# The root of the norms' column sums: one GpSimd power instruction in place of a bit trick and three Newton steps

## The chip, the cores and the metric

The kernel runs on one core of one Trainium2 chip. The metric is the device time of one execution in microseconds (us); lower is better. The core's engines work at the same time and wait for each other through semaphores: PE (TensorE, matrix products), DVE (VectorE), ACT (ScalarE), POOL (GpSimd) and SP (SyncE), which issues most transfers. POOL issues transfers too.

## The reference, cut to what matters

One inference step of a decoder layer: a prompt of 2048 tokens and 64 sample tokens, model width 1024, FFN width 2816, all in fp32. Four RMS norms frame the two sub-layers; each needs, for every token, the inverse root of the mean square of its 1024 values.

```python
def rmsnorm(x, g):
    xf = x.astype(jnp.float32)
    y = xf * lax.rsqrt(jnp.mean(xf * xf, axis=-1, keepdims=True) + EPS)
    return (y * g.astype(jnp.float32)).astype(x.dtype)

def layer(x, ...):
    xn = rmsnorm(x, g_pre_mix)
    proj = xn @ w_in                      # dilated attention and GLA heads
    ...
    x = x + rmsnorm(mixed, g_post_mix)
    f, conv_new = conv_ffn(rmsnorm(x, g_pre_ffn), conv_buf, w_up, conv_w, conv_b, w_down)
    x = x + rmsnorm(f, g_post_ffn)
```

## The kernel before

Values lie transposed: the 1024 features on 128 partitions in 8 tiles, tokens along the free axis. Every product of fp32 values is done as three matmuls on high and low parts (names ending in h and l, or hi and lo; `split`, L71, makes the low part on DVE or POOL).

The program has three parts. The sweeps (0 to about 600 us) make the projections, in four chunks `c` of 512 tokens, with the GLA heads' work woven in. Attention follows, to about 1100 us. The tail takes chunks of 528 tokens: output projection `wo`, the generator `post` (two norms for each chunk), then the FFN (`ffn`, `strassen`, `down`) and the last norm (`final` for chunks 0 to 2, `final_end` for the two halves of chunk 3, which end the program).

A norm is made in `rms_bcast`:

- the squares are summed over the 8 tiles into `ssq`, on DVE or POOL;
- PE multiplies each 128 tokens of `ssq` with a column of ones (L128; L130 adds a second summand): `pn`, one column of up to 5 values on each partition;
- `rms_cols` takes the root: DVE makes `av` (L103, named rca) = mean + EPS, then a first guess by a bit trick (L104), then three Newton steps. With `eng="v"` the steps run on DVE (L113 to L115, three instructions each); with `eng="p"` on POOL (L107 to L110, four each). The result is named rcy;
- PE transposes rcy, broadcast to 128 columns (L145): `pb`, a row of factors for all partitions. ACT or DVE copies it to SBUF (L61, L63), or it is read in place (L1734).

There are 17 such norms. Eleven have `pin=True` and took their Newton steps on POOL: two for each chunk in `post`, one each in `final` for chunks 0 to 2. Pinned means that the transposes of L145 have a fixed place in PE's order, behind a given matmul. Six have `pin=False` and took them on DVE: four in `norm_pre` (chunks 0 to 3 of the sweeps) and two in `final_end`. In chunk 0 of the sweeps the column rcy is also copied by DVE into `y0` (L668, L669), which scales later tiles. The GLA head norm in `gla_out` calls `rms_cols` by itself, always on DVE, and keeps doing so.

The order of instructions on each engine is set when the program is built, by a scheduler that works with its own estimate of durations, under the places fixed by hand (`after`, `gate`). Each engine then runs its list in order: whatever stands behind a waiting instruction waits too.

Of the kernel before, what the change touches and what calls it, by code (L numbers as in the profile page):

```python
# [10 lines left out]
F32 = mybir.dt.float32  # L11
# [3 lines left out]
ALU = mybir.AluOpType  # L15
AX = mybir.AxisListType

D = 1024
# [18 lines left out]
class Layer:  # L37
# [13 lines left out]
    def consts(self):  # L51
        nc = self.nc
        self.cp = self.ctx.enter_context(self.tc.tile_pool(name="const", bufs=1))
        self.ident = self.cload("ident", [128, 128])
        self.ones = self.cp.tile([128, 1], F32, name="c_ones")
        nc.vector.memset(self.ones, 1.0)
        self.gv = self.cload("gvec", [128, 4, KT])

    def evac(self, out, in_, eng):
# [38 lines left out]
    def rms_cols(self, ps, n, inv, nb, pool, name, eng="v"):  # L98
        nc = self.nc
        av = pool.tile([128, nb], F32, name=self.n(name + "a"), tag="rc_a", bufs=2)  # L100
        y = pool.tile([128, nb], F32, name=self.n(name + "y"), tag="rc_y", bufs=2)
        z = pool.tile([128, nb], F32, name=self.n(name + "z"), tag="rc_z", bufs=2)
        nc.vector.tensor_scalar(av[:n], ps, inv, EPS, op0=ALU.mult, op1=ALU.add)  # L103
        nc.vector.tensor_scalar(y[:n].bitcast(I32), av[:n].bitcast(I32), -0.5, 1597463007.0, op0=ALU.mult, op1=ALU.add)  # L104
        if eng == "p":
            for _ in range(3):
                nc.gpsimd.tensor_tensor(z[:n], y[:n], y[:n], op=ALU.mult)  # L107
                nc.gpsimd.tensor_tensor(z[:n], z[:n], av[:n], op=ALU.mult)
                nc.gpsimd.tensor_scalar(z[:n], z[:n], -0.5, 1.5, op0=ALU.mult, op1=ALU.add)
                nc.gpsimd.tensor_tensor(y[:n], z[:n], y[:n], op=ALU.mult)  # L110
            return y
        for _ in range(3):
            nc.vector.tensor_tensor(z[:n], y[:n], y[:n], op=ALU.mult)  # L113
            nc.vector.scalar_tensor_tensor(z[:n], z[:n], -0.5, av[:n], op0=ALU.mult, op1=ALU.mult)
            nc.vector.scalar_tensor_tensor(y[:n], z[:n], 1.5, y[:n], op0=ALU.add, op1=ALU.mult)  # L115
        return y

    def rms_bcast(self, ssq, w, out, pool, psum, tag, shape=(128, 512), bufs=None, gap=2, lead=0, eng="a", pin=False, more=None):
        nc = self.nc
        for _ in range(lead):  # L120
            yield
        nb, n = -(-w // 128), 128
        o = [min(128 * j, w - 128) for j in range(nb)]
        ps = psum.tile(list(shape), F32, name=self.n("pn"), tag=tag, bufs=bufs)
        if len(shape) == 3:
            ps = ps[:, 0, :]
        for j in range(nb):
            self.pnmm = nc.tensor.matmul(ps[:n, j:j + 1], ssq[:, o[j]:o[j] + n], self.ones, start=True, stop=more is None)  # L128
            if more is not None:
                nc.tensor.matmul(ps[:n, j:j + 1], more[:, o[j]:o[j] + n], self.ones, start=False, stop=True)  # L130
            if pin:
                self.after(self.pnmm, self.lastmm)
            self.gate("n", self.pnmm)
        y = self.rms_cols(ps[:n, :nb], n, 1.0 / D, nb, pool, "rc", "p" if pin else "v")
        self.ycol = y
        for _ in range(gap):
            yield
        for g in range(0, nb, 4):
            pb = psum.tile(list(shape), F32, name=self.n("pb"), tag=tag, bufs=bufs)
            self.pbt = pb  # L140
            if len(shape) == 3:
                pb = pb[:, 0, :]
            for j in range(g, min(g + 4, nb)):
                pm = self.lastmm
                self.pbmm = nc.tensor.transpose(pb[:, o[j] - o[g]:o[j] - o[g] + n],  # L145
                                                y[:n, j:j + 1].to_broadcast([n, 128]), self.ident)
                if pin:
                    self.after(self.pbmm, pm)
            m = o[j] - o[g] + n
            if out is not None:  # L150
                self.evac(out[:, o[g]:o[g] + m], pb[:, :m], eng)
# [1861 lines left out]
```

## Time and profile before

| What | Value |
|---|---|
| time, median of 3 runs | 2807.63 us (2795.0 to 2810.9) |
| profiled execution | 2800.35 us; its span, first to last instruction, 2798.5 us |
| granted TensorE clock over the span | 0.98 |
| PE busy | 2682.2 us (96%) |
| DVE busy | 1841.5 us (66%) |
| ACT busy | 1269.1 us (45%) |
| POOL busy | 593.4 us (21%) |

PE is busy nearly all the time, so the idle pieces of PE, some 116 us in all (2798.5 less 2682.2), are where a change on another engine can show. The profile names for each idle piece the instruction that ended it. Rows of a timeline read: start in us, length in us, engine, line, operation, output<-input, size, count, and in brackets the idle time of that engine just before, with what ended it. Buffer numbers are left out of names there.

### The profile page before, as it was taken

To read this page: it belongs to the slowest core of one execution; us is meant where nothing else is said; L and a number is where in the kernel's file an instruction comes from. 1 tells how busy PE (TensorE), PEld (TensorE's weight loads), DVE (VectorE), ACT (ScalarE), POOL (GpSimd) and SP (SyncE) were. 2 spreads that over 40 slices of the span, in tenths; PEclk is the share of its full clock that TensorE was granted. 3 is DMA by queue.
4 is the path that set the end of the run, shared out by engine and by line. 5 is a ranking of instruction groups with operands and counts; after the bars stand their busy time and mean duration, and the time that the engine had idled before them with its cause. 6 is when DMAs were issued, how large, how long until landed. Compare 5 with 4: busy or idle time off the path is not lost. (4 is left out here: it accounts for less than half of the span.)

```text
span 2798.5 us, 58530 instructions
## 1 busy us (share of the span) xinstructions
PE 2682.2 (96%) x22203; PEld 2538.9 (91%) x22203; DVE 1841.5 (66%) x4578; ACT 1269.1 (45%) x2959; POOL 593.4 (21%) x741
## 2 busy tenths in 40 slices
PE   7999999999989998998999998999999999999997
PEld 6889899788778887998899998999999999999997
DVE  7667655444357777466999888676577766666666
ACT  6535433333257776344554444434244333343332
POOL 3424242443333666013000011000020000200001
PEclk9999999999999999998999999999999999999998
DMA  8755446789798764367578677886698875976654
GB/s 302 258 177 181 168 129 208 269 329 361 269 211 174 185 165 141 102 231 254 195 275 297 224 273 291 290 297 223 211 333 282 298 237 198 328 255 215 219 186 147
DMA packets 283594, 656.82 MB, mean 235 GB/s; under 512 B 31841, under 2 KB 81633, under 8 KB 281265
## 3 DMA queue, kind: packets, MB, share of 16 engines
q1 hardware_dynamic: 253008, 574.66, 61.1%
q0 software_dynamic: 13216, 46.56, 5.1%
q10 hardware_dynamic: 17088, 31.86, 3.1%
q8 instruction: 175, 2.87, 0.4%
q14 instruction: 107, 0.87, 0.1%
HBM read 509.02 MB, written 143.94 MB: 233 GB/s over the span
## 5 line engine op out<-in xcount | busy, mean ns | idle before, releaser
L68 ACT ACTIVATE ws<-wr 128x512 fp32r<-128x512 f32 (+1 forms) x482 | 292.9, 616 | 432.4 <-PE pfe L1585 139.1
L90 PE MATMUL pfd<-hh,ws 128*128 128x264 f32 x2816 | 476.9, 286 | 8.3 <-ACT ws L68 6.7
L90 PEld LDWEIGHTS pfd<-hh,ws 128*128 128x128 f32 x2816 | 401.4, 189 | 11.2 <-ACT ws L68 8.6
L71 DVE TENSOR_TENSOR ws<-wr,ws 128x512 fp32r<-128x512 f32 (+1 forms) x482 | 320.0, 670 | 135.8 <-ACT ws L68 131.0
L90 PE MATMUL pfd<-hl,ws 128*128 128x264 f32 x1408 | 303.7, 285 | 0.0
L1585 PE MATMUL pfa<-xh,ws 128*128 128x264 f32 x1496 | 292.8, 287 | 6.8 <-ACT ws L68 2.4
L1585 PE MATMUL pfe<-xh,ws 128*128 128x264 f32 x1496 | 288.6, 285 | 4.2 <-DVE u L1572 2.9
L1585 PE MATMUL pfd<-xh,ws 128*128 128x264 f32 x1408 | 288.0, 285 | 2.8 <-DVE up L1572 2.4
L1585 PEld LDWEIGHTS pfa<-xh,ws 128*128 128x128 f32 x1496 | 237.3, 190 | 8.7 <-ACT p L1574 2.9
L1585 PEld LDWEIGHTS pfe<-xh,ws 128*128 128x128 f32 x1496 | 235.9, 189 | 4.9 <-DVE u L1572 3.3
L398 PE MATMUL pv<-wh,xh 128*128 128x256 f32 (+1 forms) x816 | 234.1, 287 | 1.1 <-DVE th L695 1.1
L1585 PEld LDWEIGHTS pfd<-xh,ws 128*128 128x128 f32 x1408 | 230.7, 189 | 3.8 <-DVE up L1572 3.0
L398 PE MATMUL pv<-wl,xh 128*128 128x256 f32 (+1 forms) x816 | 232.0, 284 | 0.0
L398 PE MATMUL pv<-wh,xl 128*128 128x256 f32 (+1 forms) x816 | 231.9, 284 | 0.0
L90 PEld LDWEIGHTS pfd<-hl,ws 128*128 128x128 f32 x1408 | 226.8, 189 | 0.1
L1534 POOL DMA_DIRECT2D xl<-d_xst x52 | 28.6, 550 | 894.5 <-PE pfe L1585 866.0
L1826 ACT ACTIVATE ass<-ass,aml 128x256 f32<-128x256 f32 (+1 forms) x384 | 173.6, 454 | 89.8 <-DVE aml L1822 88.6
L1585 PE MATMUL pfd<-xl,ws 128*128 128x264 f32 x704 | 200.2, 285 | 0.0
L90 PE MATMUL pq<-xh,wh 128*128 128x512 f32 (+2 forms) x480 | 175.4, 373 | 10.2 <-ACT xh L236 7.7
L1613 DVE TENSOR_TENSOR acc<-acc,pfd 128x264 f32<-128x264 f32 x304 | 116.7, 424 | 91.0 <-PE pfd L90 90.9
L1585 PE MATMUL pfe<-xl,ws 128*128 128x264 f32 x616 | 175.4, 285 | 0.0
L1585 PE MATMUL pfa<-xl,ws 128*128 128x264 f32 x616 | 175.2, 284 | 0.0
(341 smaller groups left out, 6691.4 us busy)
## 6 DMA issues: line engine op xcount, KB each, us to landing
ws<-d_wst SPq DMA_DIRECT2D x248, 512.0 KB
wr<-in_wu SPq DMA_DIRECT2D x114, 512.0 KB
d_wst<-ws SPq DMA_DIRECT2D x88, 512.0 KB
wr<-in_wd SPq DMA_DIRECT2D x160, 256.0 KB
wr<-in_wt SPq DMA_DIRECT2D x60, 512.0 KB
wh<-d_wbs SPq DMA_DIRECT2D x35, 512.0 KB
wl<-d_wbs SPq DMA_DIRECT2D x35, 512.0 KB
skp<-in_ckt SPq DMA_DIRECT2D x16, 1024.0 KB
```

Of the source, the lines that this page charges most:

```text
L68: h = nc.scalar.activation(hi, src, AF.Copy)
L71: return h, (nc.gpsimd if lo_eng == "p" else nc.vector).tensor_tensor(lo, src, hi.bitcast(F32), op=ALU.subtract)
L90: mm = nc.tensor.matmul(o, ww[:, k, :], xx[:, s0:s0 + n], start=(k == order[0] and i == 0), stop=(k == order[-1] and i == 2))
L398: mm = nc.tensor.matmul(ps[:m, :256], x[:, t0:t0 + m], w[:, k % 4, :], start=(k == 0 and i == 0), stop=(k == KT - 1 and i == 2))
L1534: self.nc.gpsimd.dma_start(t.bitcast(F32), xo[i, z])
L1585: self.lastmm = nc.tensor.matmul(bank[:, :H], w[:, ww, k, :], xx, start=new and k == 0 and j == 0, stop=k == 3 and j == 2, skip_group_chec ...
L1613: nc.vector.tensor_tensor(acc[m][:, s0:s0 + n], acc[m][:, s0:s0 + n], pz, op=ALU.add)
L1826: ex = nc.scalar.activation(ssb[:, sc:sc + nk], ssb[:, sc:sc + nk], AF.Exp, bias=self.ml[:, idx, h:h + 1], scale=-1.0, accum_out=self.ml[: ...
```

## The change

`consts` gets a tile of minus one half, 128x5, set once by DVE. In `rms_cols` the path for `eng="p"` becomes a single POOL instruction, av to the power of minus one half; the bit trick on DVE and the twelve POOL instructions of that path are gone. In `rms_bcast` all 17 norms now take this path, also the six that took DVE's. `z` is still allocated and not used there. Behind the edit every line number is lower by 2 (L145 becomes L143); ahead of it higher by 2 (L71 becomes L73); av moves from L103 to L105, and the power instruction is the new L107.

```diff
@@ consts
         nc.vector.memset(self.ones, 1.0)
+        self.mhalf = self.cp.tile([128, 5], F32, name="c_mhalf")
+        nc.vector.memset(self.mhalf, -0.5)
@@ rms_cols
         nc.vector.tensor_scalar(av[:n], ps, inv, EPS, op0=ALU.mult, op1=ALU.add)
+        if eng == "p":
+            nc.gpsimd.tensor_tensor(y[:n], av[:n], self.mhalf[:n, :nb], op=ALU.pow)
+            return y
         nc.vector.tensor_scalar(y[:n].bitcast(I32), av[:n].bitcast(I32), -0.5, 1597463007.0, op0=ALU.mult, op1=ALU.add)
-        if eng == "p":
-            for _ in range(3):
-                nc.gpsimd.tensor_tensor(z[:n], y[:n], y[:n], op=ALU.mult)
-                nc.gpsimd.tensor_tensor(z[:n], z[:n], av[:n], op=ALU.mult)
-                nc.gpsimd.tensor_scalar(z[:n], z[:n], -0.5, 1.5, op0=ALU.mult, op1=ALU.add)
-                nc.gpsimd.tensor_tensor(y[:n], z[:n], y[:n], op=ALU.mult)
-            return y
         for _ in range(3):
@@ rms_bcast
-        y = self.rms_cols(ps[:n, :nb], n, 1.0 / D, nb, pool, "rc", "p" if pin else "v")
+        y = self.rms_cols(ps[:n, :nb], n, 1.0 / D, nb, pool, "rc", "p")
```

Three places in the engines' lists show what moves. The first is DVE in the first norm of the sweeps (chunk 0); wl is the low part of a weight tile, pb the transposed factors, gq and gk GLA tiles that are scaled by them. Before:

```order
L113 TENSOR_TENSOR rcz_292<-rcy_291 128x4
L71 TENSOR_TENSOR wl_459<-wr_456,wh_458 128x1024
L114 SCALAR_TENSOR_TENSOR rcz_292<-rcz_292,rca_290 128x4
L115 SCALAR_TENSOR_TENSOR rcy_291<-rcz_292,rcy_291 128x4
L668 COPY y_345<-rcy_291 128x4
L669 TENSOR_SCALAR y_345<-rcy_291 128x4
L63 COPY rb_284<-pb_338 128x512
L672 SCALAR_TENSOR_TENSOR gq_258<-pq_259,rb_284 128x512
```

The same place in DVE's list after the change, from av on:

```order
L105 TENSOR_SCALAR rca_292<-pn_287 128x4
L73 TENSOR_TENSOR wl_409<-wr_406,wh_408 128x1024
L666 COPY y_338<-rcy_293 128x4
L667 TENSOR_SCALAR y_338<-rcy_293 128x4
L65 COPY rb_286<-pb_331 128x512
L670 SCALAR_TENSOR_TENSOR gq_260<-pq_261,rb_286 128x512
L670 SCALAR_TENSOR_TENSOR gk_305<-pq_306,rb_286 128x512
L614 TENSOR_TENSOR lr_343<-plr_196,rb_286 128x512
L73 TENSOR_TENSOR wl_452<-wr_449,wh_451 128x1024
```

The ten instructions of the root are gone from DVE, the copy into y now waits for POOL, and one weight split that stood among the Newton steps has moved behind lr.

The second place is POOL in `post` of chunk 2, second norm, behind a run of transfers (L1534) that POOL issues for the FFN. Before, with the four instructions of a Newton step, which follow twice more:

```order
L1534 DMA xh_16445<-d_xst 128x528
L1534 DMA xl_16446<-d_xst 128x528
L107 TENSOR_TENSOR rcz_16350<-rcy_16349 128x5
L108 TENSOR_TENSOR rcz_16350<-rcz_16350,rca_16348 128x5
L109 TENSOR_SCALAR rcz_16350<-rcz_16350 128x5
L110 TENSOR_TENSOR rcy_16349<-rcz_16350,rcy_16349 128x5
```

The same place in POOL's list after the change, where this norm and the next two take one row each:

```order
L1532 DMA xh_16339<-d_xst 128x528
L1532 DMA xl_16340<-d_xst 128x528
L107 TENSOR_TENSOR rcy_16255<-rca_16254,c_mhalf 128x5
L107 TENSOR_TENSOR rcy_16424<-rca_16423,c_mhalf 128x5
L107 TENSOR_TENSOR rcy_17508<-rca_17507,c_mhalf 128x5
L1532 DMA xl_21001<-d_xst 128x528
```

Nothing is moved across the transfers; the norm's place among them is the same.

The third place is DVE at the end of the program, where the last half of `final_end` takes its norm. Before, with the first of the three Newton steps:

```order
L1734 SCALAR_TENSOR_TENSOR acc_31930<-acc_31930,c_gvec,pb_35552 128x264
L103 TENSOR_SCALAR rca_35648<-pn_35641 128x3
L104 TENSOR_SCALAR rcy_35649<-rca_35648 128x3
L113 TENSOR_TENSOR rcz_35650<-rcy_35649 128x3
L114 SCALAR_TENSOR_TENSOR rcz_35650<-rcz_35650,rca_35648 128x3
L115 SCALAR_TENSOR_TENSOR rcy_35649<-rcz_35650,rcy_35649 128x3
```

After:

```order
L1732 SCALAR_TENSOR_TENSOR acc_31764<-acc_31764,c_gvec,pb_35377 128x264
L105 TENSOR_SCALAR rca_35473<-pn_35466 128x3
L1732 SCALAR_TENSOR_TENSOR acc_31526<-acc_31526,c_gvec,pb_35484 128x264
L1732 SCALAR_TENSOR_TENSOR acc_31560<-acc_31560,c_gvec,pb_35484 128x264
L1732 SCALAR_TENSOR_TENSOR acc_31594<-acc_31594,c_gvec,pb_35484 128x264
```

DVE goes straight from av to the scaling, and the root between them stands on POOL, behind the additions of the first half.

The lists also differ where nothing was edited, since the scheduler was run anew: on PE in parts of the sweeps (from about 40 to 200 us), and in two stretches of FFN work at the end of chunk 0's first group and about the start of chunk 1. The sum of PE's work is the same.

## The prediction

> **What bounds the kernel now.** I read the page's busy table first, then the waits of PE, then the timeline at each norm that PE waited for.
>
> ```profile
> PE 2682.2 (96%) x22203; PEld 2538.9 (91%) x22203; DVE 1841.5 (66%) x4578; ACT 1269.1 (45%) x2959; POOL 593.4 (21%) x741
> ```
>
> PE works 96% of the span, so the change can pay only in the 116 us in which PE stood (2798.5 - 2682.2), or where PE runs slow behind a pause. The waits of PE, longest first, name whom it waited for (total us, times, longest):
>
> ```profile
> PE pb L145 <- POOL rcy L110: 17.2, 3, 12.2
> ...
> PE pb L145 <- DVE rcy L115: 6.4, 2, 4.0
> ```
>
> The first is the head of that list: the transposes of a norm waiting for the POOL Newton steps. With DVE's row, 23.6 us of PE's idle time stand directly behind the root. The other twelve of the 17 norms cost PE nothing: their transposes come up when the root is long done. So the sum has five places.
>
> **The price of the power instruction** is not in this trace. The rows that bound it:
>
> ```profile
> L107 POOL TENSOR_TENSOR rcz<-rcy x33: 189/195/4187, 1154.6 to 2429.9; 128x5 f32<-128x5 f32 x33
> ...
> L71 POOL TENSOR_TENSOR wl<-wr,wh 128x1024 fp32r<-128x1024 f32 x48 | 119.2, 2489 | 168.6 <-ACT wh L68 143.1 <-DMA d_kl<-ql 9.9 <-PE pgo L941 7.0
> ```
>
> A multiplication of the same shape takes 0.195 us in the median (min/median/max in ns), so 0.2 us is the low end. As high end I take 2.5 us, the mean of a subtraction over 1024 elements for each partition: as if one power cost 200 subtractions. Twelve steps of 0.195, which made the same root, are 2.3 us, near that end, but most of a step is fixed cost, paid once in one instruction. So the value is nearer the short row: 0.8 us, an estimate. The 4187 ns maximum of L107 matters too; place 3 shows why.
>
> **The places.** 1: the first norm of the sweeps (chunk 0), which ran on DVE.
>
> ```profile
> 25.86 0.16 DVE L103 TENSOR_SCALAR rca<-pn 128x4 f32<-128x4 f32 x1 [1.82 <-PE pn L128]
> 25.94 1.23 DVE L71 TENSOR_TENSOR wl<-wr,wh 128x1024 fp32r<-128x1024 f32 x1
> ...
> 31.04 0.17 DVE L115 SCALAR_TENSOR_TENSOR rcy<-rcz,rcy 128x4 f32<-128x4 f32 x1
> ...
> 31.35 1.09 PE L145 MATMUL pb<-c_ident,rcy 128*128 128x128 f32 x4 [4.03 <-DVE rcy L115]
> ...
> 33.52 0.63 PE L90 MATMUL pq<-xh,wh 128*128 128x512 f32 x1
> 33.95 0.63 PE L90 MATMUL pq<-xl,wh 128*128 128x512 f32 x1
> ...
> 36.08 0.43 PE L90 MATMUL pq<-xh,wh 128*128 128x512 f32 x1
> ...
> 37.50 0.39 PE L90 MATMUL pq<-xh,wh 128*128 128x512 f32 x1
> 37.73 0.39 PE L90 MATMUL pq<-xl,wh 128*128 128x512 f32 x1
> ...
> 33.00:60.00 27.00, 22.90 (x127) 19.67 (x126) 18.20 (x30) 19.09 (x42) 11.37 (x13) 0.88 0.80 302
> ```
>
> (The last row is a window: its length, the busy us of PE, PEld, DVE, ACT and POOL, then the granted clock, here 0.88 against 0.98 over the span.) PE was free at 31.35 - 4.03 = 27.32. POOL can start when the split of L71 ends, 27.17 (place 3 tells why not at 26.0), so rcy is there at about 28.0 and PE starts at 28.1: 3.25 us sooner. After the 4 us pause matmuls also followed each other by 0.43 us instead of 0.23, for some nine of them until 36.08: 9 x 0.2 = 1.8 us that a pause of 0.8 us should not cost. The scheduler moved one weight split behind lr; PE reads that weight only in the products after the fourth head tile, so I price that at nothing, and if PE waited there it would be about one split, 1.23 us.
>
> 2: the two norms of `post` at 1252 and 1267 us.
>
> ```profile
> 1251.83 0.20 POOL L110 TENSOR_TENSOR rcy<-rcz,rcy 128x5 f32<-128x5 f32 x1
> 1252.08 0.52 PEld L145 LDWEIGHTS pb<-c_ident,rcy 128*128 128x128 f32 x5 [0.30 <-POOL rcy L110]
> ...
> 1261.23 0.16 DVE L103 TENSOR_SCALAR rca<-pn 128x5 f32<-128x5 f32 x1
> ...
> 1267.13 0.76 PE L145 MATMUL pb<-c_ident,rcy 128*128 128x128 f32 x5 [1.45 <-POOL rcy L110]
> ```
>
> From av (1261.39) to the transposes lie 5.7 us, and the power instruction needs under 2: both waits go, 0.30 + 1.45 = 1.75 us.
>
> 3: the longest wait.
>
> ```profile
> 1299.16 0.16 DVE L103 TENSOR_SCALAR rca<-pn 128x5 f32<-128x5 f32 x1
> ...
> 1302.24 0.17 DVE L104 TENSOR_SCALAR rcy<-rca 128x5 int32<-128x5 int32 x1
> ...
> 1305.94 0.69 DVE L71 TENSOR_TENSOR ws<-wt,ws 128x512 fp32r<-128x512 f32 x1
> 1309.51 0.69 DVE L1551 TENSOR_TENSOR wt<-wr,wr 128x512 f32<-128x512 f32 x1 [2.88 <-DMA wr<-in_wu]
> ...
> 1302.49 4.19 POOL L107 TENSOR_TENSOR rcz<-rcy 128x5 f32<-128x5 f32 x1 [1.39 <-DVE rcy L104]
> ...
> 1309.54 0.71 POOL L110 TENSOR_TENSOR rcy<-rcz,rcy 128x5 f32<-128x5 f32 x1
> ...
> 1310.31 1.33 PE L145 MATMUL pb<-c_ident,rcy 128*128 128x128 f32 x5 [12.24 <-POOL rcy L110]
> ```
>
> The first POOL step took 4.19 us, 20 times its median, and ended at 1306.68, just as DVE's unbroken run of two-input instructions ended (1305.94 + 0.69 = 1306.63). So POOL got no access while DVE ran; the same run stands between av and there in the changed list. The power instruction may start waiting at 1299.4, but ends only at 1306.63 + 0.8 = 1307.4, and of the 12.24 us PE gets back 1310.25 - 1307.45 = 2.8. The Trainium skill, GPSIMD Engine Reference, section Specifications, says that POOL shares its SBUF interfaces with DVE and suffers from DVE instructions with two SBUF inputs. By that rule the trace agrees, 4.19 us; without it POOL would be done at 1300.3 and the sum would be about 7 us better. The pause stays near 9 us, so the slow stretch of PE behind it stays too.
>
> 4: the norm of `final` for chunk 0.
>
> ```profile
> 1706.01 0.16 DVE L103 TENSOR_SCALAR rca<-pn 128x5 f32<-128x5 f32 x1
> ...
> 1707.61 1.84 POOL L107 TENSOR_TENSOR rcz<-rcy 128x5 f32<-128x5 f32 x1 [20.77 <-DVE rcy L104]
> ...
> 1717.16 1.18 POOL L110 TENSOR_TENSOR rcy<-rcz,rcy 128x5 f32<-128x5 f32 x1
> 1718.39 0.86 PE L145 MATMUL pb<-c_ident,rcy 128*128 128x128 f32 x5 [3.48 <-POOL rcy L110]
> 1719.27 0.42 PE L1585 MATMUL pfb<-xl,ws 128*128 128x264 f32 x1
> 1719.49 0.64 PE L1585 MATMUL pfb<-xh,ws 128*128 128x264 f32 x2
> ...
> 1722.35 0.29 PE L1585 MATMUL pfd<-xl,ws 128*128 128x264 f32 x1
> 1722.47 0.28 PE L1585 MATMUL pfe<-xh,ws 128*128 128x264 f32 x1
> ```
>
> Twelve short steps took 10.7 us here (1707.61 to 1718.34), again through waits of up to 1.8 us behind DVE. One instruction pays such a wait once or twice: done by about 1710, while PE comes at 1714.9. The whole 3.48 us go, and the slow matmuls after it (0.22 us apart, until 1722.35, against 0.12 from there): 16 x 0.1 = 1.6 us.
>
> 5: the end of the program.
>
> ```profile
> 2786.33 0.16 DVE L103 TENSOR_SCALAR rca<-pn 128x3 f32<-128x3 f32 x1 [1.77 <-PE pn L130]
> ...
> 2788.59 0.90 PE L145 MATMUL pb<-c_ident,rcy 128*128 128x128 f32 x3 [2.37 <-DVE rcy L115]
> ```
>
> From av's end (2786.49) to the transposes were 2.10 us. Now a hand-over to POOL (0.08, as from L104 to L107 in place 3), 0.8, and one to PE (0.05, place 2): 0.93, so 1.17 us less, straight on the path that ends the program. In the first half of `final_end` PE had matmuls to do until the root was there; nothing.
>
> The remaining removals lie beside PE's work: some 71 short DVE instructions of 0.16 us and the POOL steps of the other norms. The one DVE instruction added, a memset, stands before DVE's first input arrives. No transfer is added and none is moved past a norm; SP's list differs at about 1740 us in the order of weight loads and outputs, which I price at nothing: nothing from there is among PE's longest waits.
>
> **The sum.** Waits: 3.25 + 1.75 + 2.8 + 3.48 + 1.17 = 12.45. Slow matmuls: 1.8 + 1.6 = 3.4. Together 15.85. Some is given back, since DVE is full behind places 2 and 3:
>
> ```profile
> 1430.00:1480.00 50.00, 49.28 (x406) 49.07 (x405) 48.70 (x101) 25.99 (x47) 0.00 (x0) 1.00 0.82 294
> ```
>
> DVE is busy 48.7 of 50 us, so a PE that comes sooner waits for it: I take half of the 4.55 us of places 2 and 3, 2.3, and 0.7 of place 1, and round to 13 us net. The profiled execution took 2800.35, 7.3 under the median of 2807.63; 2800.35 - 13 = 2787, and against the median 2807.63 - 13 = 2795. With 0.2 us for the power the gain is 17.8 before giving back (0.6 less at places 1, 3 and 5 each), with 2.5 us it is 10.8 (1.7 more each).
>
> **The rivals.**
>
> *The power takes long.* POOL may work out a power by many steps for each value. Place by place, with a power of p us, against before: place 1 p - 4.05 (not under -4.0), place 2 p - 5.6 twice (not under -0.30 and -1.45), place 3 p - 3.6, place 4 p - 12.1 (not under -3.5), place 5 p - 1.97. At p = 5 they add to about +1: that is where it decides. At 10 they add to +27, without the norms that PE did not wait for, which begin to count too. I say 2835, 2807.63 + 27 (2815 to 2900). For it: no row shows a power. Against: every POOL row of five elements is short.
>
> *The gain is handed back.* Where DVE or a transfer sets the pace, PE only waits elsewhere. For: DVE's 48.7 of 50 us, and 16 us of gain in pieces of 1 to 5. Against: places 1, 4 and 5 stand where PE runs on. Then only place 5 and the larger part of place 4 remain, about 5 us: 2803.
>
> *The first power loads code.* Ahead of POOL's first tensor instruction stands a reload of its library, and that first one was slow:
>
> ```profile
> 28.78 2.21 POOL L179 TENSOR_TENSOR ssq<-ssq,sq 128x512 f32<-128x512 f32 x1 [24.03 <-ACT sq L178]
> 31.73 1.27 POOL L179 TENSOR_TENSOR ssq<-ssq,sq 128x512 f32<-128x512 f32 x1 [0.74 <-ACT sq L178]
> ```
>
> It cost 0.94 us more, with 24 idle us ahead that may have hidden the rest. In the change place 1 comes first. If a load as long as place 1's slack came on top, some 4 us, place 1 would bring nothing: 13 - 5 + 0.7, about 8 us left: 2799. The Trainium skill, GPSIMD Engine Reference, section Instruction dispatch, gives about 6 us for a first call to a freshly loaded kernel; by that figure the sum would be an estimated 5 us net. The trace's 0.94 us speaks against it.
>
> *The new order costs or brings something.* The scheduler placed its work anew in the sweeps and in two FFN stretches; the longest piece of PE idle time in the reordered part of the sweeps is this one:
>
> ```profile
> PE pkt L751 <- DVE gkh L750: 3.0, 1, 3.0
> ```
>
> Five such pieces against the kernel, with the gain handed back, make 15 us more than before: 2823. The other way they make 2780, with the gain kept.
>
> **How the numbers follow.** Forecast 0.52, handed back 0.16, long power 0.13, code load 0.05, order 0.14 (0.08 better, 0.06 worse). About 0.5% (14 us) is what a measurement can tell from no change. The forecast's own range, 4 to 18 us net, straddles that: 0.27 faster, 0.25 same. With the order's 0.08 that makes 0.35 faster; same is 0.25 + 0.16 + 0.05 = 0.46; slower 0.13 + 0.06 = 0.19. The range reaches from 2779 (17.8 and a good order, and runs as far under the median as those before) to 2826, into the long power; about 2 in 10 lie outside.
>
> **What would show it.** In the profile after: POOL's new L107, 17 times, with a median under 1 us, right; over 5 us, the forecast is wrong by the first rival. In PE's waits, pb (now L143) behind rcy at 1252, 1267 and 1718 gone, at 1310 about 9.4 us left, at 28 us under 1. PE's pause before the last transposes falls from 2.37 to about 1.2. If these go and the span stays, look for new waits of PE on ws, u or up between 1340 and 1480.

## The result and the profile after

The changed kernel takes 2791.06 us in the median of 20 runs (2783.55 to 2804.51), the kernel before 2799.3 in 20 runs beside it (2795.0 to 2810.9): 0.997 of the time before, 95% interval 0.996 to 0.9979. That is 8.2 us less, or 0.3%. It is under the 0.5% that the prediction calls the least to be told from no change, but the interval leaves out 1, so a small gain is there. The profiled execution took 2790.49 us, its span is 2788.7.

The page's busy table of the changed kernel:

```profile
PE 2680.4 (96%) x22203; PEld 2538.7 (91%) x22203; DVE 1829.6 (66%) x4508; ACT 1268.0 (45%) x2959; POOL 567.3 (20%) x626
```

The two longest of PE's waits (total us, times, longest):

```profile
PE pao L1858 <- DMA av<-out_o_vp: 16.0, 4, 8.1
PE pb L143 <- POOL rcy L107: 11.6, 3, 9.6
```

PE's busy time has hardly moved (2682.2 before), so 8.0 of the 9.8 us of span are idle time of PE. Of the 23.6 us directly behind a root 11.6 are left. A wait that was not among the longest stands first now: `av`, the attention's value tiles, loaded from DRAM.

The power instruction by its line (min/median/max in ns), and then the five places. A row that has no bracket waited less than 0.15 us.

```profile
L107 POOL TENSOR_TENSOR rcy<-rca,c_mhalf x17: 850/1256/2702, 26.8 to 2777.8; 128x5 f32<-128x5 f32 x12, 128x4 f32<-128x4 f32 x3, 128x3 f32<-128x3 f32 x2
```

Place 1 on DVE, POOL and PE:

```profile
26.60 0.16 DVE L105 TENSOR_SCALAR rca<-pn 128x4 f32<-128x4 f32 x1 [2.22 <-PE pn L126]
26.68 1.23 DVE L73 TENSOR_TENSOR wl<-wr,wh 128x1024 fp32r<-128x1024 f32 x1
...
26.85 1.95 POOL L107 TENSOR_TENSOR rcy<-rca,c_mhalf 128x4 f32<-128x4 f32 x1 [22.09 <-DVE rca L105]
...
28.85 0.65 PE L143 MATMUL pb<-c_ident,rcy 128*128 128x128 f32 x4 [0.79 <-POOL rcy L107]
```

The wait fell from 4.03 to 0.79 us. The power ran 1.95 us beside DVE's split of 1.23.

Place 2 (the second of its two norms), place 3, place 4 and place 5:

```profile
1271.95 0.76 PE L143 MATMUL pb<-c_ident,rcy 128*128 128x128 f32 x5
...
1308.20 0.54 POOL L1532 DMA_DIRECT2D xh<-d_xst  x1 [0.54 <-DMA xh<-d_xst]
1309.15 0.54 POOL L1532 DMA_DIRECT2D xl<-d_xst  x1 [0.42 <-DMA xl<-d_xst]
1309.71 2.70 POOL L107 TENSOR_TENSOR rcy<-rca,c_mhalf 128x5 f32<-128x5 f32 x1
...
1310.67 0.68 DVE L73 TENSOR_TENSOR ws<-wt,ws 128x512 fp32r<-128x512 f32 x1
...
1312.46 1.33 PE L143 MATMUL pb<-c_ident,rcy 128*128 128x128 f32 x5 [9.59 <-POOL rcy L107]
...
1705.16 2.18 POOL L107 TENSOR_TENSOR rcy<-rca,c_mhalf 128x5 f32<-128x5 f32 x1 [20.30 <-DVE rca L105]
...
2778.74 0.90 PE L143 MATMUL pb<-c_ident,rcy 128*128 128x128 f32 x3 [1.26 <-POOL rcy L107]
```

At place 3 DVE's unbroken run ended at 1311.35 (1310.67 + 0.68) and the power 1.06 us later. At place 4 the transposes came at 1713.58 and waited for nothing. The 10 us from the transposes on in the kernel before (a window: length, busy us and count of PE, PEld, DVE, ACT, POOL, then the granted clock):

```profile
1718.40:1728.40 10.00, 10.00 (x70) 10.00 (x71) 5.45 (x11) 3.41 (x7) 0.00 (x0) 0.83 0.39 143
```

And in the changed kernel:

```profile
1713.50:1723.50 10.00, 10.00 (x85) 10.00 (x85) 10.00 (x20) 5.82 (x12) 0.00 (x0) 1.00 0.85 314
```

PE is busy 10 of 10 us in both, but does 85 matmuls in place of 70: without the pause of 3.48 us the clock stays at 1.00.

### The profile page after: what moved, and what is told of

The parts are those of the page before. It is cut to its first block, busy times and chain, and to the rows that moved or that the text cites. A ratio compares the mean times of both kernels' runs of the same rounds, so it can differ in the third digit from the quotient of the medians.

```text
span 2788.7 us, 58335 instructions
## 1 busy us (share of the span) xinstructions
PE 2680.4 (96%) x22203; PEld 2538.7 (91%) x22203; DVE 1829.6 (66%) x4508; ACT 1268.0 (45%) x2959; POOL 567.3 (20%) x626
## 4 chain that ended last, share of the span: by engine, by line
PE 75%; DMA 9%; DVE 8%; POOL 3%; issue 3%; ACT 1%; SPq 1%; ACTq 0%; DVEq 0%; POOLq 0%
PE pfd L92 17%; PE pv L396 9%; PE pfa L1583 8%; PE pfe L1583 8%; PE pfd L1583 8%; PE pq L92 6%; PE pfb L1583 4%; PE pbo L1424 3%; PE pas L1815 2%; PE pao L1858 2%; PE pat L1841 1%; DVE ws L73 1%; DMA av<-out_o_vp 1%; DMA raw<-in_xp 1%; POOL aop L1222 1%
## 5 line engine op out<-in xcount | busy, mean ns | idle before, releaser
L73 DVE TENSOR_TENSOR ws<-wr,ws 128x512 fp32r<-128x512 f32 (+1 forms) x482 | 319.4, 668 | 128.1 <-ACT ws L70 124.1
L92 PE MATMUL pq<-xl,wh 128*128 128x512 f32 (+2 forms) x480 | 175.1, 366 | 0.0
```

Of the source, the lines that this page charges most:

```text
L73: return h, (nc.gpsimd if lo_eng == "p" else nc.vector).tensor_tensor(lo, src, hi.bitcast(F32), op=ALU.subtract)
L92: mm = nc.tensor.matmul(o, ww[:, k, :], xx[:, s0:s0 + n], start=(k == order[0] and i == 0), stop=(k == order[-1] and i == 2))
```

## The experiments

Two theories stood for where the rest of the gain went. In the profiled pair the first sums of `post` began 6.5 us later than before (1158.9 against 1152.4), and the end came 9.8 us earlier. A: the five places pay as the trace shows, and the attention's loss is scatter of its transfers. B: the root of the sweeps' norms makes the attention longer each time.

### The same kernel again, and each half of the change alone

The changed kernel unedited:

> The changed kernel once more, for a second profile of it. Its first profile was 6.5 us later than before at the first norm of post (1158.9 us against 1152.4), though no code of the attention was edited, and 9.8 us earlier at the end. Theory A (the five places pay, and the loss in the attention is scatter of the transfers): the first sums of post start anywhere from 1148 to 1159 us, PE's wait for av there is not again at 16 us; the time is 2791 +- 4. Theory B (the new order in the sweeps loses it each time): the first sums of post again at 1157 to 1160 us and the wait for av at 14 to 18 us.

The power for the pinned norms alone:

```diff
-        y = self.rms_cols(ps[:n, :nb], n, 1.0 / D, nb, pool, "rc", "p")
+        y = self.rms_cols(ps[:n, :nb], n, 1.0 / D, nb, pool, "rc", "p" if pin else "v")
```

> The power only for the 11 pinned norms (places 2, 3, 4); the six others keep bit trick and Newton steps on DVE. Theory A: 1 + 3 + 3.5 us and some clock, half of places 2 and 3 given back: 5 to 7 us under the kernel before, 2793. Theory B (the sweeps' part costs 6.5 us in the attention, and the rest gains what the first profile shows from 1158 us on): 13 to 16 us under it, 2785, and the first sums of post at 1150 to 1153 us.

The power for the six others alone ("q" is the old POOL path):

```diff
+        y = self.rms_cols(ps[:n, :nb], n, 1.0 / D, nb, pool, "rc", "q" if pin else "p")
```

> The power only for the six norms that ran on DVE (places 1 and 5 among them); the 11 pinned norms keep bit trick and Newton steps on POOL. Theory A: place 1 brings 2.5 us and the end 1.2, and up to 2.5 of it is lost again at 270 to 295 us as in the first profile: 1 to 4 us under the kernel before, 2796. Theory B: 5 us over it, 2804, and the first sums of post at 1157 to 1160 us.

| Kernel | median, us | ratio to before (2798.48) | first sums of `post`, us |
|---|---|---|---|
| changed, again | 2792.0 | 0.9978 (0.9967 to 0.9989) | 1157.0 |
| pinned norms only | 2791.22 | 0.9975 (0.9963 to 0.9988) | 1153.7 |
| six others only | 2800.9 | 1.0015 (1.0004 to 1.0027) | 1161.3 |

The eleven pinned norms alone bring 7.3 us, all that the whole change brings. The six others alone bring nothing (2.4 us slower), though their waits shrank. That is neither A's 1 to 4 us gain nor B's 5 us loss, and for the pinned norms A's 5 to 7 us are nearer than B's 13 to 16.

In the repeat the first sums of `post` came at 1157.0, which both theories allow. PE waited 19.2 us for `av` there, where A expected no such wait again and B 14 to 18. But that wait does not tell the theories apart: it was 13.2 us with the power on the six others alone, and 15.9 us in the kernel before with one edit at place 3 (below), which has no power at all.

Place 3 in the kernel with the power on the pinned norms alone, POOL, DVE and PE:

```profile
1300.42 0.54 POOL L1532 DMA_DIRECT2D xh<-d_xst  x1
1301.11 0.54 POOL L1532 DMA_DIRECT2D xl<-d_xst  x1 [0.15 <-issue]
1301.66 5.27 POOL L107 TENSOR_TENSOR rcy<-rca,c_mhalf 128x5 f32<-128x5 f32 x1
...
1300.96 0.68 DVE L1551 TENSOR_TENSOR wt<-wr,wr 128x512 f32<-128x512 f32 x1
...
1305.19 0.69 DVE L73 TENSOR_TENSOR ws<-wt,ws 128x512 fp32r<-128x512 f32 x1
...
1306.98 1.33 PE L143 MATMUL pb<-c_ident,rcy 128*128 128x128 f32 x5 [9.59 <-POOL rcy L107]
```

The power's own 1.2 us became 5.27: it ended at 1306.93, 1.05 us after DVE's unbroken run (1305.19 + 0.69 = 1305.88). In the changed kernel's first profile POOL's ten last transfer issues held the power up until 1309.71, and yet PE lost the same 9.59 us. So it was in four executions (changed, again, pinned norms only, and the sizes below): the power took 2.70, 4.08, 5.27 and 4.33 us as it began later or earlier, it ended 1.05 to 1.06 us behind DVE's run in all four, and PE waited 9.59 us each time. The end of DVE's run sets this wait, and the transfer issues cost nothing.

### Place 3: the transposes later

One number of the program: the generator of this norm gives way six times in place of three between the sums and the transposes, in chunk 2 only. On PE 36 FFN products then stand between them; before there were none.

```diff
-        yield from self.rms(ssq2, w, rb2, 2, 3 if c < 3 else 5, pin=True)
+        yield from self.rms(ssq2, w, rb2, 2, (3, 3, 6, 5)[c], pin=True)
```

> The changed kernel, and the transposes of the second norm of post chunk 2 (place 3) come three steps later in the program, so that 36 FFN products stand between the sums and the transposes on PE, where before nothing stood. If the pause of 9.6 us was the root's alone, the wait of PE for rcy at 1312 us goes and the kernel is 5 to 9 us faster than the changed kernel: 2784. Rival: the x operands of those products, which POOL's queue issues until 1309 us, and the weights come no sooner than the root, so PE stands just as long, now for xh, xl or ws: 2791.

Measured: 2780.95 us, 0.9938 of before (0.9924 to 0.9952), 11 us under the changed kernel on the same chip (2792.0), more than the 9.59 us of the wait. PE there:

```profile
1296.34 1.17 PE L126 MATMUL pn<-c_ones,bssq 128*128 128x1 f32 x10
1297.37 1.71 PE L1583 MATMUL pfa<-xh,ws 128*128 128x264 f32 x12
...
1302.48 0.39 PE L1583 MATMUL pfa<-xh,ws 128*128 128x264 f32 x1 [1.95 <-ACT ws L70]
...
1305.78 0.81 PE L1583 MATMUL pfa<-xh,ws 128*128 128x264 f32 x2 [2.79 <-DVE ws L73]
...
1308.14 1.15 PE L143 MATMUL pb<-c_ident,rcy 128*128 128x128 f32 x5
```

No wait for the root is left. The rival was half right: 4.74 us of waiting came back for weights. The rest of the gain is behind it. The 20 us after the transposes in the changed kernel:

```profile
1313.00:1333.00 20.00, 20.00 (x148) 20.00 (x147) 13.22 (x27) 10.79 (x19) 1.17 (x1) 0.87 0.43 153
```

And with the later transposes:

```profile
1309.00:1329.00 20.00, 20.00 (x167) 20.00 (x167) 19.20 (x39) 13.17 (x23) 1.62 (x1) 1.00 0.26 89
```

167 matmuls in place of 148, at a clock of 1.00 in place of 0.87. From the first sum of place 3 to the 50th matmul behind it PE needed 12.7 us in place of 18.1, to the 400th 55.1 in place of 65.7, to the 600th 84.0 in place of 96.7.

The same edit in the kernel before, without any power:

> The kernel before (bit trick and Newton steps everywhere), with the transposes of place 3 three steps later as in the run before. If the 36 products cover the whole root there, the 12.2 us pause goes and the kernel comes to about 2787, and then the power instruction is worth about 6 us beside that edit. Rival: the products need the same x operands that POOL issues, and the twelve POOL steps come behind all of those issues, so some 2 to 4 us of the pause stay: 2790.

Measured: 2788.65 us, 0.9961 (0.9948 to 0.9974), 9.35 us under before (2798.0). The rival's size came out:

```profile
1304.98 1.18 POOL L107 TENSOR_TENSOR rcz<-rcy 128x5 f32<-128x5 f32 x1 [0.90 <-DVE rcy L104]
...
1306.53 4.19 POOL L109 TENSOR_SCALAR rcz<-rcz 128x5 f32<-128x5 f32 x1
...
1314.58 1.33 PE L145 MATMUL pb<-c_ident,rcy 128*128 128x128 f32 x5 [3.11 <-POOL rcy L110]
```

One of the twelve steps was again held 4.19 us, and 3.11 us of PE's wait stay. The rival's cause did not show: the first step waited for DVE's bit trick (the bracket), 0.90 us behind POOL's last issue. So moving the transposes is worth about as much as the whole change (9.35 and 8.2 us), and the two add up: both together, run on two chips, have medians of six of 2780.95 and 2776.19 us, 17.5 and 21.6 under the kernel before on the same chip.

### The price of a power by size

Behind the last norm of the changed kernel POOL runs, three of each, on a scratch tile:

```diff
+            for w, op in ((5, ALU.mult), (1, ALU.pow), (5, ALU.pow), (16, ALU.pow), (64, ALU.pow), (256, ALU.pow), (512, ALU.pow), (512, ALU.mult)):
+                for _ in range(3):
+                    nc.gpsimd.tensor_tensor(B[:, :w], B[:, :w], (E if op == ALU.pow else B)[:, :w], op=op)
```

> The changed kernel, and behind its last norm POOL runs, on a scratch tile, three of each: a multiplication of 5 elements for each partition, the power of 1, 5, 16, 64, 256 and 512 elements, a multiplication of 512. The time of the program says nothing here. If the power costs a fixed part and a small part for each element, as a multiplication does, 128x1 and 128x5 are near 0.85 us and 128x512 is under 5 us. If POOL works out each value by many steps, 128x5 is some times 128x1, and 128x512 is 50 us and more.

Measured on POOL with DVE done (one row of each size; the row of two multiplications, 2.16 us, is the 512-element one):

```profile
2782.65 1.17 POOL L1755 TENSOR_TENSOR bsc<-bsc,bex 128x5 f32<-128x5 f32 x1
2785.14 2.90 POOL L1755 TENSOR_TENSOR bsc<-bsc,bex 128x16 f32<-128x16 f32 x1
2794.07 10.54 POOL L1755 TENSOR_TENSOR bsc<-bsc,bex 128x64 f32<-128x64 f32 x1
2825.94 41.23 POOL L1755 TENSOR_TENSOR bsc<-bsc,bex 128x256 f32<-128x256 f32 x1
2949.86 82.14 POOL L1755 TENSOR_TENSOR bsc<-bsc,bex 128x512 f32<-128x512 f32 x1
3197.63 2.16 POOL L1755 TENSOR_TENSOR bsc<-bsc 128x512 f32<-128x512 f32 x2
```

(82.14 - 1.17) / 507 = 0.16 us for each element of a partition, and about 0.37 us fixed. A power of 512 elements costs 82.14 us, 79 times the multiplication (1.04). A multiplication's time grows by only (1.04 - 0.195) / 507 = 0.0017 us for each element, some 95 times less. That is what was expected if POOL works out each value by many steps. The change is cheap because a norm has 3 to 5 values on a partition.

### The sweeps' norms and the attention

Here place 1 gets its old root back, or a slower power, or a shorter Newton, always with the later transposes of place 3.

Place 1 on DVE, and four powers in a row at place 1:

```diff
+        self.rcn += 1
-        y = self.rms_cols(ps[:n, :nb], n, 1.0 / D, nb, pool, "rc", "p")
+        y = self.rms_cols(ps[:n, :nb], n, 1.0 / D, nb, pool, "rc", "v" if self.rcn == 1 else "p")
```

```diff
+            for _ in range(3 if self.rcn == 1 else 0):
+                nc.gpsimd.tensor_tensor(z[:n], av[:n], self.mhalf[:n, :nb], op=ALU.pow)
             nc.gpsimd.tensor_tensor(y[:n], av[:n], self.mhalf[:n, :nb], op=ALU.pow)
```

> The changed kernel with the later transposes at place 3, and place 1 (the first norm of the sweeps) given back to bit trick and Newton steps on DVE; all other norms keep the power. The first transposes start 2.5 us later, at 30.3 to 31.5 us. Theory A (the loss in the attention is scatter): 2 to 3 us slower than the same kernel with the power there, 2783. Theory B (the sweeps' part makes the attention some 5 us longer): from the first pao group of number 28 (about 889 us) to number 80 (about 1085 us) PE needs 196 us as in the two executions without the power in the sweeps, where the four with it needed 199 to 204, and the kernel is 0 to 3 us faster: 2779.

> The changed kernel with the later transposes at place 3, and at place 1 POOL computes the power four times, three of them into a scratch tile, so the root is late by three powers (2.6 us or a little more, at 0.85 each) while the order of the sweeps stays that of the changed kernel. PE's wait for rcy at place 1: 3.4 us or more. If it is the earlier arrival that makes the attention longer, the 52 pao groups take 196 us again and the time stays at 2781. If it is the order that the scheduler chose for the sweeps, they take 199 to 204 and the time is 2783 to 2785.

Then, on one chip together: the kernel with the power everywhere, the one with place 1 on DVE, the one with the power on the pinned norms alone, and one with a single Newton step on DVE at place 1 (`range(1 if self.rcn == 1 and name == "rc" else 3)`).

> The changed kernel with the later transposes at place 3 once more, on one chip with the next three. Theory B (with the power at place 1 the sweeps' work is placed in another order, and the attention behind it takes longer): from pao group 28 to 80 PE needs 199 to 209 us again, and the time is 2781, some 3 us above the next kernel. Theory A (scatter): anything from 196 to 209, and the time 2 to 3 us below the next kernel.

> The same with place 1 on DVE by bit trick and Newton steps, once more. Theory B: 196 to 199 us from pao group 28 to 80, 2778. Theory A: 196 to 209 us, 2783.

> The later transposes at place 3, the power for the 11 pinned norms alone, all six others on DVE as before. The sweeps are in the order of the kernel before. Theory B: 196 to 199 us from pao group 28 to 80; the end lacks its 1 us: 2779. Theory A: 196 to 209 us, 2784.

> As the kernel with place 1 on DVE, but with one Newton step there in place of three, which leaves out two steps of that root. PE waits for it about 1.5 us in place of 4.0, so the sweeps run some 2.5 us earlier, and their order is a third one (that of the kernel with four powers at place 1, whose attention took 209 us). If a changed order of the sweeps is what the attention pays for: 199 to 209 us from pao group 28 to 80 and 2780 to 2784. If that is scatter: 196 to 204 us, and 2775, the 2.5 us under the kernel with three steps.

A pao group is a run of matmuls that write `pao`, the attention's products with its value tiles. The stretch is the time from the start of group 28 to that of group 80, counted from 0, in the profiled execution.

| Root at place 1 | stretch, us | median, us (with later transposes) |
|---|---|---|
| power: changed, again, six others only, later transposes, sizes, repeat | 201.5, 202.9, 204.4, 199.0, 199.1, 201.5 | 2780.95 and 2776.19 |
| DVE, three Newton steps: before, pinned only, before with later transposes, place 1 on DVE, its repeat, pinned only with later transposes | 196.3, 196.3, 199.0, 197.5, 195.7, 199.4 | 2777.6 and 2781.36; pinned only 2783.15 |
| DVE, one Newton step | 197.5 | 2777.72 |
| four powers | 209.0 | 2783.34 |

That stretch as a window, first in the repeat with the power at place 1:

```profile
885.10:1086.60 201.50, 175.32 (x1658) 153.81 (x1657) 133.32 (x612) 141.82 (x553) 140.35 (x139) 0.92 0.68 162
```

In the repeat with place 1 on DVE:

```profile
888.20:1083.90 195.70, 173.85 (x1658) 152.30 (x1657) 133.66 (x612) 141.97 (x553) 140.63 (x141) 0.93 0.71 167
```

With the power on the six others alone:

```profile
887.70:1092.00 204.30, 183.50 (x1657) 161.31 (x1656) 132.36 (x612) 142.33 (x552) 140.17 (x139) 0.88 0.68 160
```

And with four powers:

```profile
886.90:1095.90 209.00, 189.21 (x1657) 165.93 (x1656) 133.46 (x612) 142.89 (x553) 139.60 (x140) 0.86 0.66 157
```

The stretches hold B's expectation: with the power at place 1 the attention took 201.4 us in the mean of six, without it 197.4, though the ranges touch (199.0 to 204.4 and 195.7 to 199.4). In the longest of the six the granted clock was low too, 0.88 against 0.91 to 0.94 in the other five; why stays open.

The times do not hold it: on one chip the power everywhere is the fastest of the four (2776.19), 5.2 us under place 1 on DVE, where the runs before, on two different chips, had it 3.4 above. Twelve runs of each have medians of 2777.2 and 2779.4 us. So the net worth of place 1 is not settled. By three comparisons the sweeps' and the last roots brought nothing (the six others alone, 2.4 us slower than before; the whole change over the pinned norms alone, 0.8 slower; the power at place 1 over DVE there, 3.4 slower, on two chips), by the two of the last chip they brought 5.2 us (place 1) and 7.0 us (all six), more than the 4.35 and 5.5 predicted.

Two causes of the longer stretch, the earlier start of the sweeps and a changed order as such, are weakened: one Newton step made the sweeps' first transposes wait 0.7 us in place of 4.0, with a changed order of the sweeps, and the stretch stayed at 197.5. The run with four powers missed its aim: the scheduler put the needed power second of the four, so PE waited 1.78 us and not 3.4, and its 209 us are mostly a clock of 0.86, with PE busy 189.21 us.

## Why the prediction was right or wrong

The time was put at 2795, the runs gave 2791.06. The base it was taken from (2807.63, three runs) lies 8.3 us above the median of twenty, so the nearness of the two times is partly luck, and the gain is the better measure: 13 us predicted, 8.2 measured.

| Step | predicted, us | found, us |
|---|---|---|
| the power | 0.8 | 0.85, 1.01 and 1.19 for 3, 4 and 5 elements, up to 5.27 beside DVE |
| place 1, wait | 3.25 | 4.03 - 0.79 = 3.24 |
| place 1, slow matmuls | 1.8 | 7.07 - 4.84 = 2.2 (first transpose to the 20th matmul behind the transposes) |
| place 1, given back | 0.7 | 2.6 by chunk 3 of the sweeps; the rest open, see below |
| place 2 | 1.75 | 1.4: PE had waited 0.10 (the 0.30 is its weight load's) and 1.45; 0.13 is left |
| place 3 | 2.8, 9.4 left | 12.24 - 9.59 = 2.65 |
| place 4, wait and slow matmuls | 3.48 + 1.6 | 3.48 + 1.58 (to the 40th matmul, likewise: 6.88 and 5.30) |
| place 5 | 1.17 | 2.37 - 1.26 = 1.11; 2.37 - 1.65 = 0.72 in the second profile |
| given back behind places 2 and 3 | 2.3 | nothing: from the sums of place 3 to the 3000th matmul 402.6 before, 396.6 after, a gain of 6.0 |

- **The price** came out half again as high, 1.19 us for 5 elements in place of 0.8, and the median of the 17, 1.256 us, lies above the 1 us that was named as the sign of being right. The step that was off is "most of a step is fixed cost, paid once": of the power's 1.17 us only 0.37 are fixed, the rest grows with the elements. The bound of 2.5 us, "as if one power cost 200 subtractions", is passed at 16 elements (2.90); that a norm has at most 5 was the luck in it. The rival of a long power was right that the values cost much and wrong on the size.
- **Places 2, 4 and 5, and the pause at place 1,** went as read from the rows. At place 4 the slow matmuls that followed the pause of 3.48 us are gone with it. The Trainium skill, TensorE: Matmul & The Clock Gate, Part 1: The HAM clock gate, gives a warm-up of about 3.4 us of time, not of matmuls; at place 4 the trace agrees, with a granted clock of 0.50 from 1718.91 to 1722.33, 3.4 us. At places 1 and 3 of the kernel before, the clock was still 0.50 for 4.8 and 5.8 us behind the pause, more than that.
- **Place 3**: the size was right, and so was the mechanism: in four executions the power ended 1.05 to 1.06 us behind DVE's run, whenever it began. The transfer issues ahead of the power were left out, the last of which ended at 1301.10 in the kernel before. So the power could not "start waiting at 1299.4", and without DVE it would have gained some 5.5 us more by the same working, not 7. The forecast did not suffer, since DVE's run ended later.
- **The mis-sized term** is what is given back. Behind place 3 nothing was, although DVE is as full from 1430 to 1480 us as before (48.60 of 50 us). The failing step is "0.7 of place 1". From av of place 1 (25.86 before, 26.60 after) to the sums of chunk 3 (262.52 and 260.40) 236.7 us became 233.8: 2.9 of the 5.4 us were left, and the attention, on which the prediction has no step, took 5.2 us longer in that pair (196.3 and 201.5).
- **The sum by halves**: places 2 to 4 with the give-back are 1.75 + 2.8 + 3.48 + 1.6 - 2.3 = 7.3 us, and the pinned norms alone gained 7.3. The agreement is partly luck: the trace has 3.3 us more behind place 3, and the medians of one kernel on two chips differ by as much as 4.8 us (2780.95 and 2776.19). Places 1 and 5, 5.5 us in the sum, are the ones that the runs do not show reliably. Two slips in the working change little: 15.85 + 3 x 0.6 is 17.65, not 17.8, and the five places hold six norms, so eleven others cost PE nothing, not twelve.
- **The rivals**: "handed back" left 4.6 us of gain; the 8.2 measured lie between that and the forecast. In the profiled pair a part was handed back, but in the attention, not where DVE is full. "The new order" did not cost its 15 us; whether it cost some in the attention is what the runs leave open. "Loads code" did not show: at place 1 the power was POOL's first tensor instruction and ended 0.89 us behind DVE's split, and the addition after it took 1.29 us. And in the kernel with the power on pinned norms alone the first power took 1.21 us, and the same norm in the changed kernel, where it was the fifth, 1.20. The Trainium skill's 6 us for a first call (GPSIMD Engine Reference, Instruction dispatch) is on no path here, so no run shows it; in the changed kernel the two instructions that set POOL's configuration ran at 4.7 us, 22 us ahead of the first power.

## What to carry to other kernels

A shorter instruction on a side engine pays at the few places where the main engine waits for it. So list them and price each from its rows. Ask what ends the wait: where another engine's run holds the side engine, as at place 3, a shorter instruction gains little. Then look at what stands directly ahead of the consumer in the main engine's list: here ten sums were followed at once by the transposes that need their root, and putting 36 products between them brought as much as all 17 faster roots. A pause of PE costs more than its length, since the matmuls behind it run at a lower clock for some us. Where a gain stands ahead of a stretch set by transfers, don't count it as kept until runs of that part alone show it.

## What the runs showed of the hardware

- GpSimd's power costs about 0.37 us and 0.16 us for each element of a partition: 0.57 for one, 1.17 for 5, 82.14 for 512.
- A POOL instruction of 1.2 us was held 5.27 us beside back-to-back DVE instructions with two inputs, and one of 0.2 us 4.19 us, both to about the end of DVE's run. In four executions the power began up to 2.6 us apart, as seen from that end, and ended 1.05 to 1.06 us behind it each time.
- Behind a pause of 3.48 us PE needed 6.88 us from the first transpose to the 40th matmul behind the transposes, without the pause 5.30. Behind one of 4.03 us it needed 7.07 us to the 20th, behind one of 0.79 us 4.84.
